# Second sums of a seven written over its raw page, a seventh raw slot, and new constants for the order

## Chip, cores and metric

The kernel runs on one core of one Trainium2 chip. The metric is the device time of one execution in microseconds. Three runs of the kernel before took 2598.05 to 2601.19 us, with a median of 2599.41 us.

## What is computed

Two layers of an encoder over 256 tokens of width 4096, all in float32. Each layer normalises its input, multiplies it by one wide input projection (4096 x 11264), runs grouped attention with rotary embedding on one half of the result and a retention in both directions on the other half, gates both, and multiplies by an output projection (4096 x 4096), which is added to the input. A last normalisation ends it.

```python
for l in range(DEPTH):                       # DEPTH = 2
    h = rmsnorm(x, norm_w[l])
    proj = h @ w_in[l]                       # 256 x 4096 @ 4096 x 11264
    aq, ak, av, ag, rq, rk, rv, rg = jnp.split(proj, SPLIT_POINTS, axis=-1)
    ...
    a_out = (jax.nn.silu(ag) * gqa_attention(aq, ak, av)).astype(x.dtype)
    ...
    r_out = (jax.nn.silu(rg.astype(jnp.float32)) * r).astype(x.dtype)
    x = x + jnp.concatenate([a_out, r_out], axis=-1) @ w_out[l]
return rmsnorm(x, final_norm)
```

## The kernel before

**Products.** Each float32 value is split into a high part and a low part of a shorter type (fp32r): ScalarE (ACT) casts the high part, VectorE (DVE) subtracts it from the value to get the low part. A product is then three matmuls: high by high, low operand by high weight, high operand by low weight. In the profile, `whi` and `wlo` are the parts of a page of weights, and `x8h`, `x8l`, `x7h`, `x7l` those of the operand.

**Blocks.** The work runs in 30 blocks, each over two column groups of 512 (11 of the input projection and 4 of the output projection in each layer). They are numbered from 0; blocks 0, 11, 15 and 26 open the four stages (input and output projection of both layers). In a block, the 4096 rows of the weights are taken in 16 pairs of 2 x 128. Most pairs are "eights" and need eight products of 128 x 128 by 128 x 512 on two pages of weights. Six pairs of each block are "sevens": they use a Strassen-like scheme with seven products, for which sums of the weights are made on the core (`SEVENS`, L130; `SEVEN_PRODUCTS`, L192 on).

**Pages of a seven.** A seven has four pages, used in the order A, T, B, U, with pages of eights between them:
- A is the raw page (`wraw`), loaded from HBM: two halves of 512 columns.
- T is `wv`: a copy of the raw page by ACT, to which a DMA of GpSimd's queue (POOL) adds a prepared array (`add_up`, L690; `add`, L726).
- B is a half page, `third`, loaded from HBM on SyncE's queue (SP) (`load_third`, L546).
- U is `wu`: two sums by DVE. The first is the raw page's second half plus the first half of `wv`; the second is the first sum plus `third`. They are made when page T begins (`begin`, L636), into a tile of their own with one buffer.

Each page is then split: `parts` (L602) casts the high part and leaves the low part to be done later (`low`, kept in `later`); what is given as `then` is called once the low part is issued.

**Raw slots.** There are `RAWS` = 6 slots of 128 x 1024 float32 for raw pages. `load` (L524) puts the next raw page in the oldest free slot, by a DMA on SP's queue (L531). `empty` (L541) hands a slot back and calls `load`. The page of an eight hands its slot back after its low part, the A page of a seven after the second sum of `wu`. At the start all slots are filled before the third chunk of `xT` is loaded (`first_rows`, L1933, called in the opening). Casts are kept in a ring of 5 pages (`RING`), low parts in 4 (`LOWS`).

**Order.** The order of all instructions on each engine is fixed when the program is built: a planner written in the kernel keeps a clock of its own (`Now`, `Clock`, L293 on) with assumed costs and decides, after each product, which splits, loads and steps of the side work (attention, retention, gates, sums, residuals, operand splits) come next (`tick`, L1067; `room`, L731; `Lane`, L977; `block`, L1543). Its constants stand in `BASE` and, for single blocks, in `PLANS` (L111); `assume` (L124) sets those of a block. In `block` the constant `RUSH` is read first, and only if the block is called as hurried (the first of an output projection), and `assume` is called for the block after that.

Of the kernel before, what the change touches and what calls it, by code (L numbers as in the profile page):

```python
# [17 lines left out]
P = 128  # L18
# [9 lines left out]
NB = 512  # L28
# [5 lines left out]
BLK = 32  # L34
ALL = slice(None)
PAGES = 13
RAWS = 6
A_EARLY = 0
SUMS = 2
LOWS = 4  # L40
# [4 lines left out]
STRICT = 4  # L45
RELIEF = 1.5
# [6 lines left out]
STEP_V = 2.0  # L53
STEP_S = 1.5

V_FIXED = 0.1
STT = 0.0
S_FIXED = 0.2

MM = {512: 0.2268, 256: 0.1177}  # L60
PASS = 0.2
# [4 lines left out]
MARGIN = 0.2  # L66
# [4 lines left out]
ADD_SLACK = 0.3  # L71
RAW_SLACK = 0.3
U_SLACK = 0.3
THIRD_SLACK = 0.3
SUM_SLACK = 0.3

RUSH = 1.0

EARLY = 1.3
# [5 lines left out]
PE_REST = 1.5  # L85

TIGHT_A = 2
TIGHT_B = 9

AT_ONCE = 2  # L90
# [9 lines left out]
LOW_AHEAD = 1.5  # L100
LONG = 4
NEAR = 30
# [6 lines left out]
)  # L109
BASE = {_n: globals()[_n] for _n in TUNED}  # L110
PLANS = {  # L111
    1: {'LOW_AHEAD': 5.0},
    6: {'TIGHT_A': 8},
    7: {'SUM_SLACK': 0.0, 'AT_ONCE': 1, 'STRICT': 4},
    8: {'TIGHT_B': 5, 'STRICT': 5},
    9: {'THIRD_SLACK': 1.0, 'BANK_REST': 1.5, 'LOW_AHEAD': 1.0, 'RAW_SLACK': 1.0, 'RELIEF': 0.7, 'PASS': 0.1},
    14: {'STRICT': 9, 'TIGHT_A': 0},
    15: {'S_FIXED': 0.16, 'LONG': 2, 'EARLY': 1.8, 'PASS': 0.3, 'PE_REST': 2.0, 'NEAR': 30},
    22: {'PASS': 0.3, 'U_SLACK': 1.0, 'AT_ONCE': 1},
    24: {'V_FIXED': 0.12, 'TIGHT_B': 20, 'TIGHT_A': 2},  # L120
}


# [169 lines left out]
class Now:  # L293


    t = 0.0
# [40 lines left out]
def hybrid_encoder(  # L337
# [21 lines left out]
    wp = ctx.enter_context(tc.tile_pool(name="wp", bufs=3))  # L359
# [12 lines left out]
    def t(pool, shape, tag, bufs=None, dt=F32):  # L372
        kw = {} if bufs is None else {"bufs": bufs}
        return pool.tile(shape, dt, tag=tag, name=tag, **kw)
# [106 lines left out]
    class Weights:  # L481


        def __init__(self):
# [29 lines left out]
            for i, g in enumerate(self.raws):  # L514
                if g.seven and i > RAWS + A_EARLY:
                    self.raws.insert(i - A_EARLY, self.raws.pop(i))
            self.slots = [f"wraw{_i}" for _i in range(RAWS)]
            self.placed, self.emptied, self.made = 0, 0, 0
# [117 lines left out]
        def begin(self, g):  # L636

            g.begun = True
            if not g.seven:
                ac.after(g.raw_at)  # L640
                self.parts(g, g.raw, then=partial(self.empty, g))
                return
            o = g.own
            if g.kind == PAGE_A:
                self.wanted = max(self.wanted, self.sevens.index(o) + 1)
                self.load_third()
                ac.after(o.a_at)
                self.parts(g, o.a)
            elif g.kind == PAGE_T:
                self.sums_low(PAGE_A)  # L650
                self.sums_low(PAGE_U)
                self.add_up(o)
                self.add(True)
                u = o.u = t(wp, [P, 2, NB], "wu", 1)
                ve.after(max(o.v_at, o.b_at))
                ve.tensor_add(u[:, 0, :], o.a[:, 1, :], o.v[:, 0, :])
                ve.tensor_add(u[:, 1, :], u[:, 0, :], o.b)
                o.u_at = ve.until
                self.empty(next(v for v in self.seq if v.own is o))
                ac.after(o.v_at)  # L660
                self.parts(g, o.v, then=self.spend)
                self.halve()
            else:
                ac.after(o.u_at)
                self.parts(g, o.u)

        def third_split(self):
            self.split_thirds += 1
# [1427 lines left out]
```

## Time and profile before

| | |
|---|---|
| median of 3 runs | 2599.41 us |
| the profiled execution's own time | 2599.34 us |
| its span in the trace | 2597.6 us |
| granted clock | 0.998 |
| DMA | 653.52 MB, 252 GB/s in the mean |

The profile names engines PE (TensorE matmul), PEld (its weight loads), DVE, ACT, POOL and SP. A row of a group reads: line, engine, operation, tile written from tiles read, shapes, count, busy time and mean time of one. L321 is the planner's recorder, through which all operations of DVE and ACT pass, so one goes by tiles there. A row of waits reads: engine, line and tile that waited, what ended the wait, then the sum in us, how often, and the longest. A matmul's end is modelled in the trace: two that follow each other overlap, so the distance from start to start tells the rate, not the length of one.

### The profile page before, as it was taken

To read this page: it belongs to the slowest core of one execution; us is meant where nothing else is said; L and a number is where in the kernel's file an instruction comes from. 1 tells how busy PE (TensorE), PEld (TensorE's weight loads), DVE (VectorE), ACT (ScalarE), POOL (GpSimd) and SP (SyncE) were. 2 spreads that over 40 slices of the span, in tenths; PEclk is the share of its full clock that TensorE was granted. 3 is DMA by queue.
4 is the path that set the end of the run, shared out by engine and by line. 5 is a ranking of instruction groups with operands and counts; after the bars stand their busy time and mean duration, and the time that the engine had idled before them with its cause. 6 is when DMAs were issued, how large, how long until landed. Compare 5 with 4: busy or idle time off the path is not lost.

```text
span 2597.6 us, 34368 instructions
## 1 busy us (share of the span) xinstructions
PE 2581.8 (99%) x11560; PEld 2135.2 (82%) x11560; DVE 2215.3 (85%) x2710; ACT 1853.6 (71%) x2626; POOL 398.6 (15%) x548
## 2 busy tenths in 40 slices
PE   9999999999999999999999999999999999999998
PEld 7888888888888888888878888888888888888886
DVE  7898888888789898777979888889888798987777
ACT  8877777766666788656887667776666667886655
POOL 0111221221102100211111112221201021000000
PEclk9999999999999999999999999999999999999999
DMA  9988988888778778988888879888887787788886
GB/s 314 305 237 277 289 242 254 281 247 263 221 220 260 230 235 227 271 269 248 275 253 261 250 239 279 246 270 268 259 257 222 208 259 242 220 229 251 250 243 194
DMA packets 206594, 653.52 MB, mean 252 GB/s; under 512 B 24784, under 2 KB 31440, under 8 KB 206416
## 3 DMA queue, kind: packets, MB, share of 16 engines
q1 hardware_dynamic: 147040, 472.99, 51.8%
q0 software_dynamic: 58656, 177.24, 30.7%
q8 instruction: 90, 1.47, 0.2%
q10 hardware_dynamic: 720, 1.10, 0.1%
q14 instruction: 88, 0.72, 0.1%
HBM read 607.19 MB, written 44.04 MB: 251 GB/s over the span
## 4 chain that ended last, share of the span: by engine, by line
PE 94%; DMA 2%; DVE 2%; ACT 1%; issue 1%; SPq 0%; DVEq 0%; POOLq 0%; POOL 0%; ACTq 0%
PE M L1683 60%; PE M L1693 30%; PE M L1158 1%; PE M L1157 1%; PE M L1156 1%; DMA ca<-in_x 1%; DVE wlo L321 1%; ACT whi L321 1%; DMA third<-in_w_out 0%; PE M L1677 0%; DMA wraw<-in_w_out 0%; DVE cb L321 0%; DMA whole<-in_w_in 0%; ACT ca L321 0%; DVE ca L321 0%
## 5 line engine op out<-in xcount | busy, mean ns | idle before, releaser
L321 DVE TENSOR_TENSOR wlo<-wraw,whi 128x1024 fp32r<-128x1024 f32 (+1 forms) x774 | 935.3, 1215 | 172.8 <-issue 61.2
L321 ACT CAST whi<-wraw 128x1024 fp32r<-128x1024 f32 (+1 forms) x776 | 800.1, 1045 | 297.1 <-PE M L1683 283.0
L1683 PE MATMUL M<-whi,x8h 128*128 128x512 f32 x2368 | 922.5, 390 | 1.0 <-DVE cb L321 0.8
L1683 PE MATMUL M<-whi,x8l 128*128 128x512 f32 x2368 | 921.8, 389 | 0.0
L1693 PE MATMUL M<-wlo,x8h 128*128 128x512 f32 x2364 | 676.3, 389 | 0.2 <-DVE wlo L321 0.2
L1683 PEld LDWEIGHTS M<-whi,x8h 128*128 128x128 f32 x2368 | 444.6, 188 | 94.9 <-DVE cb L321 1.5
L1683 PEld LDWEIGHTS M<-whi,x8l 128*128 128x128 f32 x2368 | 444.6, 188 | 92.4 <-DVE x8l L321 0.3
L1693 PEld LDWEIGHTS M<-wlo,x8h 128*128 128x128 f32 x2364 | 442.2, 188 | 91.4 <-DVE wlo L321 1.0
L1683 PE MATMUL M<-whi,x7h 128*128 128x512 f32 x1080 | 420.5, 389 | 0.2 <-ACT whi L321 0.2
L1683 PE MATMUL M<-whi,x7l 128*128 128x512 f32 x1080 | 420.3, 389 | 0.0
L1693 PE MATMUL M<-wlo,x7h 128*128 128x512 f32 x1080 | 334.4, 390 | 0.7 <-DVE wlo L321 0.6
L729 POOL DMA_DIRECT2D wv<-in_twice_in x132 | 118.5, 898 | 1068.6 <-ACT wv L321 923.8
L321 ACT CAST whi<-wu 128x1024 fp32r<-128x1024 f32 x180 | 189.3, 1052 | 91.9 <-DVE wu L321 54.2
L321 ACT CAST whi<-wv 128x1024 fp32r<-128x1024 f32 x180 | 189.0, 1050 | 91.5 <-PE M L1683 51.9
L321 DVE TENSOR_TENSOR wlo<-wv,whi 128x1024 fp32r<-128x1024 f32 x180 | 219.6, 1220 | 37.3 <-PE M L1693 30.7
L321 ACT COPY wv<-wraw 128x1024 f32<-128x1024 f32 x180 | 188.9, 1049 | 74.7 <-DMA wraw<-in_w_out 35.2
L321 DVE TENSOR_TENSOR wlo<-wu,whi 128x1024 fp32r<-128x1024 f32 x180 | 219.1, 1217 | 24.8 <-PE M L1693 16.7
L1693 PEld LDWEIGHTS M<-wlo,x7h 128*128 128x128 f32 x1080 | 202.4, 188 | 44.1 <-DVE wlo L321 2.5
L1683 PEld LDWEIGHTS M<-whi,x7h 128*128 128x128 f32 x1080 | 202.8, 188 | 42.6 <-ACT whi L321 0.9
L1683 PEld LDWEIGHTS M<-whi,x7l 128*128 128x128 f32 x1080 | 202.8, 188 | 41.8
L321 DVE TENSOR_TENSOR wu<-wu,third 128x512 f32<-128x512 f32 x180 | 124.6, 692 | 7.0 <-DMA third<-in_w_in 0.8
L321 DVE TENSOR_TENSOR wu<-wraw,wv 128x512 f32<-128x512 f32 x180 | 123.1, 684 | 8.7 <-DMA wv<-in_twice_in 6.3
(249 smaller groups left out, 2292.0 us busy)
## 6 DMA issues: line engine op xcount, KB each, us to landing
wraw<-in_w_in SPq DMA_DIRECT2D x568, 512.0 KB, 5.2
wraw<-in_w_out SPq DMA_DIRECT2D x208, 512.0 KB, 5.4
wv<-in_twice_in POOLq DMA_DIRECT2D x132, 512.0 KB, 7.5
third<-in_w_in SPq DMA_DIRECT2D x132, 256.0 KB, 5.8
wv<-in_twice_out POOLq DMA_DIRECT2D x48, 512.0 KB, 8.1
third<-in_w_out SPq DMA_DIRECT2D x48, 256.0 KB, 5.7
full<-next_dram POOLq DMA_DIRECT2D x18, 512.0 KB, 9.5
p_dram<-room POOLq DMA_DIRECT2D x64, 128.0 KB, 3.4
```

What stands on the lines that cost most here:

```text
L321: return call(out, *args, **kwargs)
L729: self.adds.pop(0)[1]()
L1156: nc.tensor.matmul(out, a[0], b[0], start=start, stop=False)
L1157: nc.tensor.matmul(out, a[0], b[1], start=False, stop=False)
L1158: nc.tensor.matmul(out, a[1], b[0], start=False, stop=stop)
L1683: nc.tensor.matmul(acc[name], a[i], g.hi[h], start=m == first[name] and not i, stop=False)
L1693: nc.tensor.matmul(acc[name], a, g.lo[h], start=False, stop=m == final[name])
```

## The change

The two sums of page U are written into the raw page of the same seven; the tile `wu` is gone. The first sum overwrites the raw page's first half and reads its second, the second sum overwrites the second half. The raw slot of the seven is handed back after the low part of page U, no longer after the second sum. `RAWS` goes from 6 to 7, so that the raw slots take the room that the tile `wu` had. The constants of the planner for single blocks are others for blocks 0, 1, 3, 10, 11, 15, 17, 18, 25 and 26; blocks 6, 7, 8, 9, 14, 22 and 24 keep theirs, and the rest have the base.

```diff
-RAWS = 6
+RAWS = 7
...
 PLANS = {
-    1: {'LOW_AHEAD': 5.0},
+    0: {'EARLY': 1.8, 'RELIEF': 0.7, 'TIGHT_A': 2, 'RAW_SLACK': 0.3},
+    1: {'LOW_AHEAD': 3.0, 'ADD_SLACK': 1.0, 'SUM_SLACK': 0.0, 'U_SLACK': 0.3, 'NEAR': 30},
+    3: {'EARLY': 0.8, 'RAW_SLACK': 3.0},
...
+    10: {'NEAR': 30, 'RAW_SLACK': 0.3, 'STRICT': 6, 'AT_ONCE': 1, 'PE_REST': 2.5, 'THIRD_SLACK': 0.3, 'V_FIXED': 0.12, 'STEP_V': 2.5, 'PASS': 0.2, 'TIGHT_A': 8, 'MARGIN': 0.0},
+    11: {'EARLY': 1.3, 'S_FIXED': 0.18},
     14: {'STRICT': 9, 'TIGHT_A': 0},
-    15: {'S_FIXED': 0.16, 'LONG': 2, 'EARLY': 1.8, 'PASS': 0.3, 'PE_REST': 2.0, 'NEAR': 30},
+    15: {'RUSH': 0.0},
+    17: {'V_FIXED': 0.12},
+    18: {'U_SLACK': 1.0, 'STEP_S': 1.0},
...
+    25: {'STEP_S': 1.0, 'RAW_SLACK': 0.3, 'TIGHT_A': 0, 'SUM_SLACK': 1.0},
+    26: {'NEAR': 40, 'STT': 0.05, 'LONG': 0, 'THIRD_SLACK': 0.3, 'SUM_SLACK': 0.0, 'TIGHT_A': 0, 'EARLY': 1.3, 'V_FIXED': 0.1, 'PASS': 0.2},
 }
...
             elif g.kind == PAGE_T:
...
-                u = o.u = t(wp, [P, 2, NB], "wu", 1)
+                u = o.u = o.a
                 ve.after(max(o.v_at, o.b_at))
                 ve.tensor_add(u[:, 0, :], o.a[:, 1, :], o.v[:, 0, :])
                 ve.tensor_add(u[:, 1, :], u[:, 0, :], o.b)
                 o.u_at = ve.until
-                self.empty(next(v for v in self.seq if v.own is o))
                 ac.after(o.v_at)
                 self.parts(g, o.v, then=self.spend)
                 self.halve()
             else:
                 ac.after(o.u_at)
-                self.parts(g, o.u)
+                self.parts(g, o.u, then=partial(self.empty, next(v for v in self.seq if v.own is o)))
```

## Prediction

> **What bounds the kernel now.** I read the page's totals first, then the chain that ended last, then a table of PE by stretches, and only then who waits for whom.
>
> ```profile
> span 2597.6 us, 34368 instructions
> PE 2581.8 (99%) x11560; PEld 2135.2 (82%) x11560; DVE 2215.3 (85%) x2710; ACT 1853.6 (71%) x2626; POOL 398.6 (15%) x548
> PE 94%; DMA 2%; DVE 2%; ACT 1%; issue 1%; SPq 0%; DVEq 0%; POOLq 0%; POOL 0%; ACTq 0%
> ```
>
> TensorE is busy for 2581.8 of 2597.6 us and holds 94% of the chain. A busy PE isn't yet a PE at its peak, so the next look is at the rate: one piece of the chain, and from the windows view the stretches that matter (columns: PE, weight loads, DVE, ACT, POOL, each with its count, then the granted clock, the DMA share and GB/s).
>
> ```profile
> 1350.74 1.81 PE M L1683 x8
> 0.00:88.00 88.00, 86.29 (x351) 65.10 (x352) 71.42 (x103) 74.29 (x116) 5.56 (x10) 1.00 0.92 310
> 953.00:1040.00 87.00, 87.00 (x400) 72.59 (x399) 77.62 (x104) 72.55 (x115) 6.72 (x8) 1.00 0.76 218
> 1127.00:1214.00 87.00, 87.00 (x385) 72.04 (x384) 68.35 (x72) 53.04 (x61) 14.41 (x20) 1.00 0.86 258
> 1214.00:1300.00 86.00, 85.55 (x376) 69.99 (x375) 75.40 (x104) 70.47 (x114) 17.12 (x25) 1.00 0.91 287
> 1300.00:1390.00 90.00, 88.90 (x385) 71.45 (x384) 74.97 (x95) 72.47 (x114) 11.03 (x14) 1.00 0.85 250
> 2248.00:2335.00 87.00, 87.00 (x396) 72.15 (x395) 78.76 (x106) 71.07 (x111) 9.05 (x9) 1.00 0.75 220
> 2510.00:2572.00 62.00, 61.39 (x271) 50.39 (x270) 49.27 (x58) 41.27 (x58) 4.36 (x5) 1.00 0.84 250
> ```
>
> Eight matmuls took 1.81 us, 0.2267 us each. In 1127:1214, 385 matmuls touch the stretch, some 1.5 of them only over its edges: 383.5 x 0.2267 = 86.9 of 87 us, so nothing is lost there. The same count gives, for 1300:1390, 383.5 x 0.2267 = 86.9 of 90 us, **3.1 us lost**; for 1214:1300, 374.5 x 0.2267 = 84.9 of 86, **1.1 us lost**; for 2510:2572, 269.5 x 0.2267 = 61.1 of 62, **0.9 us lost**. Outside the first 88 us and the tail, that is all I find: 5.1 us. Few of them show as waits of PE with a name:
>
> ```profile
> PE M L1693 <- DVE wlo L321: 0.8, 2, 0.6
> PE M L1683 <- DVE cb L321: 0.8, 1, 0.8
> PE M L1683 <- DVE ca L321: 0.2, 1, 0.2
> PE M L1683 <- ACT whi L321: 0.2, 1, 0.2
> ```
>
> So TensorE waits for splits (whi, wlo) and for bank sums (ca, cb), never for a raw page directly. The change touches no matmul, so **5.1 us is about what it can win** in the stretches above, 0.196% of 2599.34 us, the profiled execution's time, which is 0.07 us off the median of 2599.41. The execution lies 1.7 us over its span, and I keep that.
>
> **The change part by part.** The sums come first. Two rows of the view of their tile (ns least, median, most; first and last start), and one of the waits:
>
> ```profile
> L321 DVE TENSOR_TENSOR wu<-wraw,wv x180: 651/684/694, 26.8 to 2564.6; 128x512 f32<-128x512 f32 x180
> L321 DVE TENSOR_TENSOR wlo<-wu,whi x180: 1180/1218/1228, 31.7 to 2570.1; 128x1024 fp32r<-128x1024 f32 x180
> ...
> DVE wu L321 <- DMA wv<-in_twice_in: 6.3, 4, 2.7
> ```
>
> Nothing is removed or added in number: 2 x 180 sums, 180 casts, 180 lows stay, with the same shapes. I cost the sums' new place at 0: they run on DVE behind the A page's low, and their input wv comes from a copy that ACT made of the same raw page, so every reader of the raw page is done when the sum may start anyway. The old wait that goes is that of a new wu for the cast and the low of the last one; what the sums do wait for is wv's landing (the last row, 6.3 us in all, from the view of waits), and that stays.
>
> What moves is the **raw load that follows a seven**. Before, its slot comes free after the second sum; now after the U page's low. From the first and the last row (26.8 to 31.7 + 1.2, and 2564.6 to 2570.1 + 1.2) the room is taken for 6.1 and 6.7 us, about 6.4 x 180 = 1150 us, 44% of the span if the ones between are alike. In that time there are six slots for raw pages as before, in the rest seven. The wait it adds stands on SP's queue, in front of the next raw and third loads:
>
> ```profile
> SPq L531 <- DVE wlo L321: 1343.6, 541, 7.9
> SPq L531 <- DVE wu L321: 606.3, 175, 9.0
> wraw<-in_w_in SPq DMA_DIRECT2D x568, 512.0 KB, 5.2
> wraw<-in_w_out SPq DMA_DIRECT2D x208, 512.0 KB, 5.4
> ```
>
> SP already waits for DVE before nearly every load, and the load is issued in the program where its release is, so the 175 waits for a sum become waits for a low, later on both sides. 776 loads in 2597.6 us are one in 3.35 us; six slots turn round in 20.1 us, seven in 23.4. A load lands in 5.2 to 5.4 us. The gain is up to 3.35 us of earlier issue for a raw page that comes late. Who feels a late one:
>
> ```profile
> ACT wv L321 <- DMA wraw<-in_w_out: 35.2, 17, 6.4
> ACT wv L321 <- DMA wraw<-in_w_in: 32.9, 25, 3.8
> ACT whi L321 <- PE M L1683: 362.0, 393, 3.9
> DVE wlo L321 <- PE M L1693: 95.8, 122, 1.6
> ```
>
> ACT waited 68.1 us for raw pages in all, but 362.0 us in 393 waits for TensorE to free a cast: over the span the casts run to the end of their ring, which hides late raws. Not so where TensorE loses time (ACT's waits in 1214:1300, 1300:1390, 1390:1476, 2510:2572; each fence a window):
>
> ```profile
> ACT wv L321 <- DMA wraw<-in_w_out: 7.0, 3, 4.2
> ACT whi L321 <- PE M L1683: 3.7, 4, 2.5
> ```
> ```profile
> ACT whi L321 <- PE M L1683: 3.0, 3, 2.1
> ACT wv L321 <- DMA wraw<-in_w_in: 0.9, 1, 0.9
> ```
> ```profile
> ACT whi L321 <- PE M L1683: 18.1, 21, 3.9
> ```
> ```profile
> ACT wv L321 <- DMA wraw<-in_w_out: 8.5, 3, 6.4
> ACT whi L321 <- PE M L1683: 5.1, 7, 2.3
> ```
>
> In the first and the last of them raws were late by 7.0 and 8.5 us with little ring ahead; in 1300:1390 they were not. So the seventh slot can win between 0 and 0.9 + 1.1 = 2.0 us. For the last stretch I take all 0.9: its longest wait of 6.4 us halves with 3.35 us. For 1214:1300 I take 0.5 of 1.1, since DVE is busy for 75.4 of 86 us there. **Term: -1.4 us.** What is late next in both is DVE's own turn.
>
> The slots are also filled at the start, by one more load ahead of the third chunk of xT.
>
> ```profile
> 6.16 3.54 SPq L531 DMA_DIRECT2D wraw<-in_w_in  x4
> 10.64 1.61 SPq L1937 DMA_DIRECT2D full<-in_xT  x2
> 21.50 0.90 ACT L321 ACTIVATE full<-full,nw 128x256 f32<-128x256 f32 x2
> ```
>
> At 310 GB/s of the first stretch 512 KB cost 1.7 us. The chunk is first scaled at 21.50, and TensorE is then still in the two native pairs and pairs 3 and 2. **Bounds 0 to +1.7 us; I take 0**, because about 9 us of matmuls (two pairs) lie between; without them it costs the 1.7.
>
> A rule speaks against the extra load: the Trainium skill, "DMA: Bandwidth & Descriptors", section "Queues, rings and completion order", says that each DMA engine takes turns between the queues that have work. By it a further raw load on SP's queue slows the accumulations and residuals of POOL's queue, and the sum would be that of the contention rival below. No row here separates the queues' turns.
>
> The **orders**: new constants for blocks 0, 1, 3, 10, 11, 15, 17, 18, 25, 26. Block 15's own five go; what comes, RUSH, is read before the block's constants are set and only in hurried blocks, so block 15 runs on the base. Blocks 0, 11, 15 and 26 open the four stages, and there the splits of the operand share ACT and DVE with those of the weights. What an order costs, 1300:1390 shows:
>
> ```profile
> 1328.76 0.82 ACT L321 COPY ca<-room 32x256 f32<-32x256 f32 x2
> 1329.60 1.05 ACT L321 CAST whi<-wu 128x1024 fp32r<-128x1024 f32 x1
> 1330.69 1.23 DVE L321 TENSOR_TENSOR wlo<-wu,whi 128x1024 fp32r<-128x1024 f32 x1 [1.44 <-ACT whi L321]
> 1382.15 0.50 PE L1683 MATMUL M<-whi,x8h 128*128 128x512 f32 x1 [0.80 <-DVE cb L321]
> ```
>
> Pieces of 0.4 us went ahead of a cast that TensorE needed. A new order can take these 3.1 us away or bring as many at another opening: bounds -3.1 and, per opening, +3.1. Nearest is the row itself, a stretch that is as full as before: I take 0. Sum: 2599.34 - 1.4 = **2597.9 us**.
>
> **Rivals.** *No relief:* the lost time is DVE's and ACT's crowding, not raws; four of PE's named waits are all on them. Then 2599.3, or up to 2601.0 with the start's 1.7. *All of it goes:* 2599.34 - 5.1 = 2594.2; for it, no named wait of TensorE is over 0.8 us; against it, DVE and ACT stand at 83% and 81% in 1300:1390. *Contention:* POOL's transfers land later by one load's 1.7 us where TensorE has no ring ahead, once in 1214:1390: 2601.0. Against it, the bytes stay the same. *Slower, by the openings:* the new orders put operand splits ahead of the weights' at openings that lose nothing now (953:1040 and 2248:2335 are 87.00 of 87). Each that becomes like 1300:1390 costs 3.1 us; one more is +3.1 (2602.4), from two on, +6.2 (2605.5), it is over the bound, all three (blocks 0, 11, 26) give 2608.6. For it: ACT there is busy for 72.55 and 71.07 of 87 us, as full as in 1300:1390. Against it: they lost nothing under a like load.
>
> By the Trainium skill, "TensorE: Matmul & The Clock Gate", section "HAM oscillation — how this bites in real kernels", an idle stretch of TensorE beyond some 3.4 us drops its clock to half, so that a loss of an opening in one piece would cost more than its length. The granted clock is 1.00 in all rows above, with no wait over 0.8 us, so no run here shows it.
>
> **How the numbers follow.** Forecast (2595.5 to 2599): 0.45. No relief (to 2602): 0.20. Contention: 0.08. All of it goes (2594.2 to 2595.5): 0.08. Slower by the openings: 0.16. Faster than the 5.1 us allow, by a shorter start or tail too: 0.03. A measurement can tell about 0.2%, 5.2 us, from no change, so the first four are "same": 0.81; slower 0.16, faster 0.03. The range leaves out the last two: 2594.2 to 2604.6, from the 5.1 us won to just over one opening lost with the start's 1.7 (2604.1).
>
> **What would show it.** Right: PE 99% with 11560 matmuls; the wait of ACT for in_w_out raws in the last stretch well under 8.5 us and the stretch's loss near 0; first sums with wraw as output, 180 of some 684 ns; SP's waits for a sum gone, waits for wlo up. Wrong on orders: a stretch of 87 us around 953 or 2248 with some 14 matmuls too few. Wrong on the start: a gap of PE between 26 and 40 us. The prediction falls if TensorE's time per matmul moves, or if stretches that lost nothing now lose more than 5 us together.

## The result, and the profile after

| | median, us | runs |
|---|---|---|
| before | 2599.25 | 13, 2597.41 to 2601.19 |
| after | 2604.76 | 13, 2603.00 to 2606.91 |

The ratio is **1.0022, interval 1.0014 to 1.0030**: the change costs about 5.5 us, where 1.4 us less were forecast. The profiled execution's span went from 2597.6 to 2603.0 us, so it shows the whole of the loss.

The page of the kernel after: span, busy times, and the shares of the chain that ended last.

```profile
span 2603.0 us, 34347 instructions
PE 2583.7 (99%) x11560; PEld 2134.8 (82%) x11560; DVE 2225.5 (85%) x2710; ACT 1854.9 (71%) x2627; POOL 396.5 (15%) x548
PE 94%; DVE 2%; DMA 2%; ACT 1%; issue 1%; SPq 0%; POOL 0%; POOLq 0%; DVEq 0%; ACTq 0%
L329 DVE TENSOR_TENSOR wraw<-wraw,third 128x512 f32<-128x512 f32 x180 | 124.6, 692 | 9.3 <-DMA third<-in_w_in 3.2
L329 DVE TENSOR_TENSOR wraw<-wraw,wv 128x512 f32<-128x512 f32 x180 | 123.9, 688 | 4.2
```

Nothing here tells where 5.4 us went. PE is 99% busy as before, and its busy time grew by 1.9 us only; the work is the same 11560 matmuls. The two sums are there with their new output, at 688 and 692 ns each, as in a tile of their own. The stretches tell more, by the count of matmuls as in the prediction.

Windows view of the kernel after, the same stretches as before (columns: PE, weight loads, DVE, ACT, POOL, granted clock, DMA share, GB/s):

```profile
0.00:88.00 88.00, 85.16 (x339) 62.55 (x340) 68.62 (x100) 72.14 (x115) 5.53 (x10) 1.00 0.90 299
953.00:1040.00 87.00, 87.00 (x402) 72.72 (x401) 78.42 (x109) 73.43 (x120) 6.67 (x8) 1.00 0.74 214
1214.00:1300.00 86.00, 85.67 (x375) 69.67 (x374) 74.46 (x104) 69.77 (x112) 16.16 (x23) 1.00 0.93 288
1300.00:1390.00 90.00, 85.75 (x373) 69.12 (x372) 73.66 (x93) 71.31 (x116) 8.90 (x11) 1.00 0.84 236
2248.00:2335.00 87.00, 87.00 (x398) 72.10 (x397) 77.83 (x104) 72.08 (x114) 6.71 (x8) 1.00 0.75 217
2510.00:2572.00 62.00, 62.00 (x275) 51.36 (x274) 48.61 (x55) 41.67 (x55) 6.07 (x7) 1.00 0.91 265
```

The first 88 us hold 339 matmuls in place of 351: 12 x 0.2267 = **2.7 us**. In 1300:1390 it is (373 - 1.5) x 0.2267 = 84.2 of 90 us, **5.8 us lost** in place of 3.1. The openings of blocks 11 and 26, around 953 and 2248, lost nothing. In 2510:2572 the loss seems gone (ACT's waits for raw pages there fell from 8.5 to 4.9 us), but it only moved past the edge, to a wait at 2577 (below).

The waits of PE in the kernel after, the whole span (engine, line and tile that waited, what ended it, sum, times, longest):

```profile
PE M L1690 <- ACT x8h L329: 2.5, 1, 2.5
PE M L1700 <- DVE wlo L329: 2.2, 5, 1.0
PE M L1690 <- ACT whi L329: 1.5, 1, 1.5
```

Before, no named wait of TensorE for a split or a sum was over 0.8 us; now two single ones are 2.5 and 1.5. The timeline of the kernel after places them (start, length, engine, line, operation; in brackets the idle time before it and who ended it):

```profile
22.83 0.91 ACT L329 ACTIVATE full<-full,nw 128x256 f32<-128x256 f32 x2 [1.04 <-DMA full<-in_xT]
...
42.79 0.73 PE L1700 MATMUL M<-wlo,x7h 128*128 128x512 f32 x2 [1.04 <-DVE wlo L329]
...
1316.32 1.05 ACT L329 COPY wv<-wraw 128x1024 f32<-128x1024 f32 x1 [4.85 <-DMA wraw<-in_w_in]
1317.28 1.04 ACT L329 CAST whi<-wraw 128x1024 fp32r<-128x1024 f32 x1
1318.37 0.50 PE L1690 MATMUL M<-whi,x8h 128*128 128x512 f32 x1 [1.53 <-ACT whi L329]
...
1366.53 1.65 ACT L329 COPY cb<-room 32x256 f32<-32x256 f32 x4
...
1370.62 1.04 ACT L329 CAST whi<-wraw 128x1024 fp32r<-128x1024 f32 x1
...
1372.38 0.70 ACT L329 CAST x8h<-cb 128x256 fp32r<-128x256 f32 x2
1373.13 0.51 PE L1690 MATMUL M<-whi,x8h 128*128 128x512 f32 x1 [2.47 <-ACT x8h L329]
...
2577.33 0.73 PE L1700 MATMUL M<-wlo,x7h 128*128 128x512 f32 x2 [0.57 <-DVE wlo L329]
```

Two places, then. **At the start** the scaling of the third chunk of xT begins at 22.83 in place of 21.50 us, and ACT idles 1.04 us for its landing; some 20 us later TensorE waits for the low parts. By the starts of the matmuls 0.5 us is lost between 29 and 34 us, 1.3 at 42.79, 0.5 at 56 and 0.3 around 75. **At the layer boundary** ACT stands 4.85 us in front of a copy to wv, because the raw page has not landed, and the cast that TensorE needs is queued behind that copy: TensorE stops for 1.53 us. From 1366.53 on four copies to cb and then four casts of weights, the last at 1370.62, go ahead of the operand's cast x8h: TensorE stops for 2.47 us. In the kernel before, x8h goes ahead of those four casts; its timeline there:

```profile
1365.20 0.70 ACT L321 CAST x8h<-cb 128x256 fp32r<-128x256 f32 x2
1367.22 1.05 ACT L321 CAST whi<-wraw 128x1024 fp32r<-128x1024 f32 x1
```

The first of the two waits at the boundary is led back by the chain of the kernel after, cut to 1295:1320:

```profile
1304.93 11.31 DMA wraw<-in_w_in
...
1316.32 0.04 ACT wv L329
```

A raw load issued at 1304.93 took 11.31 us; the median of all raw loads of this kernel is 5.2 to 5.3. At this place long ones are usual: of the raw loads in 1290:1320 the median is 6.2 and the longest is this one, and before they were 6.6 and 10.6. So the landing alone isn't the cause, but that the copy which waits for it has a needed cast behind it. The planner counts with 6.0 us from its estimate of the issue (`RAW_LANDING`); the copy and the cast behind it were placed by that belief.

As a ruler for all that follows I use the start of the same-numbered matmul in each trace (a matmul of one number is the same product in all kernels), less that of before:

```
matmul   before, us   after
   360        90.08   +2.84
  5000      1117.51   +2.82
  5700      1276.17   +3.33
  6000      1346.95   +4.28
  6250      1404.99   +5.93
 11000      2457.60   +6.11
 11559      2585.32   +5.97
```

So 2.8 us are lost in the first 90 us, 0.5 by 1276, another 2.6 by 1405, and from there on nothing that counts. One trace of each kernel carries this. For one kernel traced twice (e5 and e11 below) the ruler's readings differed by up to 0.6 us, so a step smaller than that isn't read from one trace alone. The ruler also holds time in which TensorE's clock was halved behind a wait (last section): the traces of e1, e2, e3, e4, e9 and e12 have such stretches, those of before, after, e5 to e8, e10 and e11 have none before the last matmuls.

### The profile page after: what moved, and what is told of

Read it like the earlier page. It is cut to its first block, busy times and chain, and to the rows that moved or that the text cites. A ratio compares the mean times of both kernels' runs of the same rounds, so it can differ in the third digit from the quotient of the medians.

```text
span 2603.0 us, 34347 instructions
## 1 busy us (share of the span) xinstructions
PE 2583.7 (99%) x11560; PEld 2134.8 (82%) x11560; DVE 2225.5 (85%) x2710; ACT 1854.9 (71%) x2627; POOL 396.5 (15%) x548
## 4 chain that ended last, share of the span: by engine, by line
PE 94%; DVE 2%; DMA 2%; ACT 1%; issue 1%; SPq 0%; POOL 0%; POOLq 0%; DVEq 0%; ACTq 0%
PE M L1690 61%; PE M L1700 30%; DMA wraw<-in_w_in 1%; PE M L1165 1%; PE M L1164 1%; PE M L1163 1%; DVE wlo L329 1%; ACT whi L329 1%; DMA full<-in_xT 0%; DVE cb L329 0%; DVE ca L329 0%; ACT cb L329 0%; DVE xf L329 0%; ACT full L329 0%; DVE x7l L329 0%
## 5 line engine op out<-in xcount | busy, mean ns | idle before, releaser
L329 DVE TENSOR_TENSOR wlo<-wraw,whi 128x1024 fp32r<-128x1024 f32 x954 | 1148.9, 1216 | 197.0 <-PE M L1700 75.3
L329 ACT CAST whi<-wraw 128x1024 fp32r<-128x1024 f32 x956 | 983.7, 1046 | 389.5 <-PE M L1690 308.5
L329 DVE TENSOR_TENSOR wraw<-wraw,third 128x512 f32<-128x512 f32 x180 | 124.6, 692 | 9.3 <-DMA third<-in_w_in 3.2
L329 DVE TENSOR_TENSOR wraw<-wraw,wv 128x512 f32<-128x512 f32 x180 | 123.9, 688 | 4.2
L329 ACT CAST bhi<-third 128x512 fp32r<-128x512 f32 x180 | 111.3, 618 | 20.3 <-PE M L1690 15.1
L329 DVE TENSOR_TENSOR blo<-third,bhi 128x512 fp32r<-128x512 f32 x180 | 123.1, 684 | 0.0
```

Source lines behind the costliest of these rows:

```text
L329: return call(out, *args, **kwargs)
```

## The experiments

Four parts of the change can carry the loss: the sums' place (in the raw page), the longer hold of the slot, the extra load ahead of xT, and the order that the planner makes from seven slots and new constants. The theory after the result was: the extra load at the start, and the order at block 15. Its rivals were the slots' traffic in general and the constants alone.

**e1: the third xT chunk ahead of the seventh raw.** Only SP's order changes.

```diff
-    while weights.slots:
+    while len(weights.slots) > 1:
         weights.load()
     first_rows(2)
+    weights.load()
```

> The changed kernel, with the third chunk of xT loaded ahead of the seventh raw page at the start and nothing else moved on any engine. Theory A (the start's 2.8 us come from the extra load ahead of xT): ACT no longer idles 1.04 us for the chunk at 22.8 us, the first 90 us come back to those of before, time 2602.0 us. Theory B (they come from the new order of block 0): the chunk lands earlier but TensorE still loses 2.8 us by 90 us, time 2604.8 us.

Measured: 2605.41 us, ratio 1.0025 (1.0015 to 1.0036). That is theory B's time: no gain, and the ruler reads +2.77 at matmul 360, as in the kernel after. The timeline of e1 tells why:

```profile
21.62 0.91 ACT L329 ACTIVATE full<-full,nw 128x256 f32<-128x256 f32 x2
29.26 0.69 DVE L329 TENSOR_TENSOR wraw<-wraw,third 128x512 f32<-128x512 f32 x1 [1.61 <-DMA third<-in_w_in]
```

The scaling is back at 21.62, but the raw load now stands ahead of the next thing in that queue, the first third, and DVE waits 1.61 us for it. The lateness was passed on, not removed. e1 thus doesn't speak against the load as the cause; e8 asks the question better.

**e2 and e3: code and constants apart.** e2 is the code of after with the `PLANS` of before, e3 the code of before with the `PLANS` of after.

```diff
 e2, in the code of after
-    0: {'EARLY': 1.8, 'RELIEF': 0.7, 'TIGHT_A': 2, 'RAW_SLACK': 0.3},
-    1: {'LOW_AHEAD': 3.0, 'ADD_SLACK': 1.0, 'SUM_SLACK': 0.0, 'U_SLACK': 0.3, 'NEAR': 30},
+    1: {'LOW_AHEAD': 5.0},
...
-    15: {'RUSH': 0.0},
+    15: {'S_FIXED': 0.16, 'LONG': 2, 'EARLY': 1.8, 'PASS': 0.3, 'PE_REST': 2.0, 'NEAR': 30},
...
```

> The changed kernel (sums in the raw page, seven slots) with the constants of before. Theory A (start from the load, layer boundary from the new constants of blocks 14 to 15): the start still loses 2 to 3 us, 1214 to 1390 us loses some 4 us as before and not 7, time 2602 us. Theory B (all from the orders): 2599 us. Theory C (all from the slots): 2604.8 us.

> The kernel before (tile wu, six slots) with the new constants. Theory A (start from the load, boundary from the constants): nothing lost at the start, 3 us more than before lost around 1300 us, time 2602 us. Theory B (all from the orders): 2604.8 us. Theory C (all from the slots): 2599.3 us.

Measured: e2 2615.67 us, ratio 1.0065 (1.0048 to 1.0082); e3 2607.20 us, ratio 1.0033 (1.0019 to 1.0046). Each half alone is slower than before, e2 is the slowest kernel of all, and no theory had either time. Where e2 loses, the windows view of e2 and its waits of PE say:

```profile
953.00:1040.00 87.00, 83.88 (x376) 69.26 (x375) 75.20 (x106) 70.78 (x113) 6.71 (x8) 0.98 0.71 209
1300.00:1390.00 90.00, 84.49 (x362) 67.22 (x363) 71.64 (x92) 73.68 (x118) 9.53 (x12) 1.00 0.81 233
2248.00:2335.00 87.00, 83.97 (x379) 69.19 (x378) 76.46 (x107) 70.94 (x116) 6.70 (x8) 0.98 0.73 206
```
```profile
PE M L1682 <- ACT whi L321: 3.9, 2, 2.8
PE M L1682 <- DVE ca L321: 2.9, 2, 2.6
PE M L1692 <- DVE blo L321: 2.1, 1, 2.1
```

376 in place of 400 matmuls around 953 (24 x 0.2267 = 5.4 us) and 362 in place of 385 in 1300:1390 (5.2 us). In 2248:2335 17 are missing against before, 3.9 us. In the first and the last of these stretches TensorE also ran at half clock for 3.4 us behind a wait; 8 matmuls touch such a piece where 16 fit, so up to 1.8 us of each loss is the clock's. The new constants thus repair, around blocks 11 and 26, what the planner does worse once it is told of seven slots and a later release. They are no gain in themselves: with six slots, in e3, they cost 8 to 9 us. Part of that lies at the start: at matmul 360 the ruler reads +4.97 in e3, and +3.90 in e10 (below), which has the same order and no halved clock there. Neither has an extra load at the start.

**e4: block 15's old constants in the kernel after.**

```diff
-    15: {'RUSH': 0.0},
+    15: {'S_FIXED': 0.16, 'LONG': 2, 'EARLY': 1.8, 'PASS': 0.3, 'PE_REST': 2.0, 'NEAR': 30},
```

> The changed kernel with the old constants of block 15 alone. Theory A1 (block 15 on the base puts casts, residual work and operand splits in a worse order): the two waits of TensorE at 1317 and 1371 us, 4.3 us, shrink to under 2 us, time 2602 us. Theory A2 (it is the late landing of one raw page at 1316 us, made before block 15's constants matter): both stay, time 2604.8 us.

Measured: 2605.13 us, ratio 1.0023 (1.0013 to 1.0033), no change against after. The ruler reads +2.81 at 5700, +7.64 at 6000 and +7.99 at 6250: the same place loses more. Part of that is the clock: the wait for whi is 2.9 us here, and behind it TensorE ran at half clock for 6.8 us. Block 15's constants alone aren't the cure.

**e5, e6, e7: the slots without a new order.** The kernel before, with its order kept on every engine: the planner is told of six slots and books its loads as before, while the program has seven. The sums go into the raw page. The load behind a seven is issued where it stood, but into the spare slot, which the last seven's page U has left, so it waits for no sum. In e6 each load goes out as soon as a slot is free, one page ahead of the planner's booking, and the seventh ahead of xT, as in the kernel after; in e7 only from the first release on. SP's own order in e5 is that of before too.

```diff
+LOGICAL = 6
...
+        def fill(self):
+            while self.slots and self.put < min(self.placed + self.ahead, len(self.raws)):
+                g = self.raws[self.put]
...
+                nc.sync.dma_start(g.raw, g.src)
...
-                u = o.u = t(wp, [P, 2, NB], "wu", 1)
+                u = o.u = o.a
...
-                self.empty(next(v for v in self.seq if v.own is o))
+                self.load()
...
-                self.parts(g, o.u)
+                self.parts(g, o.u, then=partial(self.spare, next(v for v in self.seq if v.own is o)))
...
 e6, in the opening
+    weights.ahead = 1
+    weights.fill()
     first_rows(2)
```

> Sums in the raw page and seven slots, but every instruction of every engine in the order of the kernel before: the planner is told of six slots and each load is issued where it was, into the slot that the last seven's sums left. Theory D (writing in place costs nothing; the loss comes from the order that the planner makes when it sees seven slots): 2599.3 us, at most 1 us off, nothing lost at the start or at the openings beyond before. Theory E (in place costs something by itself, by waits of the sums or the later release): 2601 to 2605 us, spread over the span.

> As the run before it, but each raw load is issued as soon as a slot is free, up to one page ahead of the order of before, the seventh ahead of the third chunk of xT; PE, ACT, DVE and POOL keep the order of before. Theory F (the extra load in flight delays what lands behind it: xT, thirds, accumulations): 2 to 3 us lost by 90 us, time 2601.5 to 2602 us. Theory D (order alone): 2599.3 us. The hope of the change (late raws were what cost): under 2598.5 us, with the loss of 2510 to 2572 us gone.

> As e6, but six raw loads at the start, and the page ahead only from the first release on. Theory F at the start alone: the first 90 us as before and the rest as in e6, time under 2599.5 us. Theory D: 2599.3 us, same as e5 and e6.

Measured: e5 **2595.86 us, ratio 0.9989** (0.9980 to 0.9998); e6 2598.50, ratio 0.9999 (0.9990 to 1.0008); e7 2597.86, ratio 0.9995 (0.9986 to 1.0004). Sums in place and a seventh slot are thus worth 3 us if the order stays and each load keeps its place in the queue, a gain that neither theory on e5 had. To fetch a page ahead in addition gives most of it back: neither e6 nor e7 can be told from before, and e7's median is 2.0 us over e5's, though the intervals of the ratios overlap. By the ruler e6 stands 1.8 us behind e5 at matmul 4230 (+1.46 in place of -0.31), of which some 1.0 were lost around 170 us, and 3.9 behind at the end. A window and a wait of ACT in e6, in 160:180:

```profile
160.00:180.00 20.00, 19.56 (x86) 15.54 (x85) 19.83 (x31) 13.61 (x23) 2.69 (x2) 1.00 0.62 193
```
```profile
ACT bhi L322 <- DMA third<-in_w_in: 1.4, 1, 1.4
```

ACT waits for a third page, issued at 152.66, to which the chain of e6 leads the loss back; 90 matmuls stood there before, 86 now. That the raw loads ahead of it in SP's queue made it late is likely, not shown: e7 fetches ahead too and lost nothing there.

Where e5 wins shows in SP's waits in 1290:1330, of before and of e5:

```profile
SPq L531 <- DVE wu L321: 22.3, 4, 9.0
SPq L531 <- DVE wlo L321: 17.3, 7, 4.4
```
```profile
SPq L542 <- DVE wlo L322: 32.8, 9, 10.1
```

The waits for a sum, 22.3 us, are gone, and those for a low part grew from 17.3 to 32.8, so that SP waits 32.8 us for the two in place of 39.6. Over the whole span SP's queue is hardly freer: it waits for wlo, wu and blo for 2027.5 us before and for 1975.3 in e5. What moves is when single loads go out. One load as an example, in the timelines of before and of e5:

```profile
1297.22 0.33 SPq L531 DMA_DIRECT2D wraw<-in_w_in  x1
```
```profile
1290.33 0.33 SPq L542 DMA_DIRECT2D wraw<-in_w_in  x1
```

It goes out 6.9 us earlier. The windows view of e5 answers:

```profile
1214.00:1300.00 86.00, 86.00 (x381) 71.25 (x380) 76.84 (x107) 70.42 (x114) 18.42 (x25) 1.00 0.92 290
1300.00:1390.00 90.00, 89.98 (x396) 73.87 (x395) 76.46 (x95) 74.87 (x116) 10.56 (x14) 1.00 0.85 250
2510.00:2572.00 62.00, 61.98 (x273) 50.97 (x272) 52.01 (x62) 40.49 (x55) 3.49 (x4) 1.00 0.71 219
```

In 1300:1390 the loss falls from 3.1 to 90 - (396 - 1.5) x 0.2267 = 0.6 us. The same pieces of ca and cb stand ahead of the same casts as before; the casts in front of them were done earlier, so TensorE had more in hand. Whether it is the earlier page itself that helps, or the loads behind it in the queue, no run separates.

**e8: the seventh page later, in the kernel after.** Its DMA is held back until just before the next raw load, so behind two chunks of xT and the first third. PE, ACT, DVE and POOL keep the order of after.

```diff
+                if self.placed == RAWS:
+                    self.held_back = g
+                else:
+                    self.bring()
+                    nc.sync.dma_start(g.raw, g.src)
```

> The changed kernel with the seventh raw page of the start loaded behind two chunks of xT and the first third; PE, ACT, DVE and POOL keep the changed kernel's order. Theory F (what lands behind the extra load is late, and that is the start's loss; in e1 the lateness only passed from xT to the third): under 1 us lost by 90 us against before, time 2602.5 us. Theory D (the order of block 0 loses them, whatever lands when): 2 to 3 us lost by 90 us as before, time 2604.8 us.

Measured: 2603.93 us, ratio 1.0017 (1.0008 to 1.0026). The intervals of e8 and after overlap, so the time alone doesn't carry it; the trace does. Its timeline at the place of the 22.83 above:

```profile
21.22 0.91 ACT L329 ACTIVATE full<-full,nw 128x256 f32<-128x256 f32 x2
```

The scaling starts 1.61 us earlier, and the ruler reads +1.17 in place of +2.84 at matmul 360. **1.7 us of the start are the extra load**; the other 1.2 stay with no load in the way, and are left to the order of block 0. Other traces repeat both: with the load in its place e4 and e9 read +2.71 and +2.73, without it e12 reads +1.21. The 1.2 us come in steps at 42, 56 and 75 us, and the first two, of 0.4 to 0.7 us each, stand also in e3 and e10, which have the new constants of block 0 and no extra load.

With the order of before, in e6, the same extra load costs 0.4 to 0.7 us by matmul 360 (+0.43, where e7, e11 and e5 read +0.04, -0.07 and -0.31). There the scaling starts at 21.99, only 0.5 to 0.8 us later than in those three. So in both orders TensorE loses about what the chunk is late; why it is less late in e6 isn't shown.

**e9: the copy to wv later, in block 15 of the kernel after.** The copy is planned 3 us behind the believed landing, so the casts behind it pass it; 14 rows of ACT move and some five of DVE, none of PE.

```diff
+SUM_LATE = 0.0
...
-    15: {'RUSH': 0.0},
+    15: {'SUM_LATE': 3.0},
...
-                elif not o.a or o.a_at > now.t or ...
+                elif not o.a or o.a_at + SUM_LATE > now.t or ...
```

> The changed kernel; in block 15 ACT takes the copy of a seven's raw page only 3 us after the planner believes that it landed, so that a late page does not stop the casts behind the copy. ACT's order changes in some 14 rows around 1310 to 1370 us, PE's not at all. Theory G (ACT standing 4.9 us at 1316 us for one raw page sets the waits at 1317 and 1371 us): both shrink, 2 to 4 us come back, time 2601 to 2603 us. Theory H (ACT and DVE are simply full there): the wait moves to another cast or operand, time 2604 to 2605 us.

Measured: 2604.25 us, ratio 1.0017 (1.0008 to 1.0027). The waits of PE in e9:

```profile
PE M L1691 <- ACT x8h L330: 2.7, 1, 2.7
PE M L1701 <- DVE wlo L330: 1.6, 3, 1.1
```

By the time alone that is theory H. But the wait for whi (1.53 us) is gone, and the ruler falls to +0.34 at matmul 6000, 3.9 us better than after: 1.8 of that are there at matmul 5800, ahead of the copy, and 1.9 more come by 5900, behind it. At 6250 it is +3.82 again, 2.1 better than after: the next wait, for x8h, grew from 2.5 to 2.7 us, and TensorE's clock was halved behind it (last section). So the queueing at 1316 is shown as a cause in the trace, of some 2 us, and e12 repeats it against e8 (2.2 us between matmuls 5800 and 5900); the wait for x8h takes back 1.8. The copies to cb don't make that wait in e9, where the last of them end at 1361.03. Its timeline shows what stands ahead of x8h, four casts of weights from here on, the first of which waited for a landing:

```profile
1363.98 1.05 ACT L330 CAST whi<-wv 128x1024 fp32r<-128x1024 f32 x1 [0.94 <-DMA wv<-in_twice_in]
...
1368.63 0.71 ACT L330 CAST x8h<-cb 128x256 fp32r<-128x256 f32 x2
```

The place of x8h behind the casts of weights is what e9 and the kernel after share; no run moved x8h alone.

**e10: the order of e3 with the edit of e5.** A new order, six slots in the planner's mind, sums in place. e10 and e3 differ as e5 and before do.

```diff
 in the code of e3
-RAWS = 6
+RAWS = 7
+LOGICAL = 6
...
-                u = o.u = t(wp, [P, 2, NB], "wu", 1)
+                u = o.u = o.a
...
```

> The order of e3 (six-slot planner, new constants) with sums in the raw page and the load behind a seven issued into the spare slot at once, as e5 did for the order of before. Theory J (that a load need not wait for the sums is worth something in any order): 1.5 to 4 us under e3's 2607.2, time 2603 to 2605.7 us. Theory K (e5's gain is peculiar to the order of before): 2607 us.

Measured: 2603.56 us, ratio 1.0017 (1.0008 to 1.0026), against 1.0033 for e3. That is theory J: sums in the raw page and loads that need not wait for a sum gain 0.16%, about 4 us (the intervals of the two ratios overlap at their ends; the ruler reads +4.48 against +9.22 at matmul 11559, but e3's trace has two stretches at half clock in that and e10's none). The order of e3, with all that, stays 4 us behind before and 8 behind e5.

**e11: e5 once more**, since it is the only kernel that is faster than before.

> e5 a second time, beside the runs above: theory D with loads that no longer wait for sums: 2595.9 us, 2 to 4 us under before; had e5's gain been chance, 2599 us.

Measured: **2595.68 us, ratio 0.9984** (0.9975 to 0.9993). The gain holds, 3 to 4 us.

**e12: e8 and e9 together.** If start and boundary are two causes, their gains add up.

> The changed kernel with both local edits: the seventh raw page of the start loaded behind the first third (e8), and the copies of block 15 taken 3 us later (e9). If the start's late landings and the copy that waits for a late page are separate causes, their gains in the traces add, 1.7 us by 90 us and 2.4 us at the layer boundary: 2604.8 - 4.1 = 2600.7 us, and what is left above before (the order of block 0, the operand split that comes late at 1367 us) is still there. If a delay at the start only shifts the same wait, 2603 to 2604 us.

Measured: 2602.24 us, ratio 1.0013 (1.0004 to 1.0022). The median is 2.8 us over before in place of after's 5.5, between the two theories; the intervals still overlap. In the traces the gains add: +1.21 at matmul 360 (after +2.84, e8 +1.17), -0.47 at 6000 (after +4.28), and a span of 2599.4 us, 3.6 below after's, where e8 alone gave 0.9 and e9 alone 2.3. The halved clock at the x8h wait is there again.

## Why the prediction was wrong

**What bounds the kernel** held: TensorE's time per matmul didn't move, and the losses were found as missing matmuls in single stretches. The condition under which the prediction was to fall came near: the first 88 us lost 2.7 us more than before, and 1300:1390, which had lost 3.1, another 2.7.

**The sums at no cost** held: 180 at 688 and 180 at 692 ns, against 684 and 692 before; e5, with its sums in the raw page, is no slower; and SP's waits for a sum became waits for a low part, as forecast (1343.6 + 606.3 us for the two before). The longest row of SP's waits in the kernel after:

```profile
SPq L539 <- DVE wlo L329: 1828.9, 715, 9.6
```

**The term of the later raws**, -1.4 us, had the right sign, and its size hangs on when the loads go out. With the order kept and a page fetched ahead, e7, without the start's load, stands 0.05% under before, some 1.3 us, which can't be told from 0 or from -1.4. With each load in its old place e5 and e11 measured -3 and -4 us (0.11% and 0.16% of 2599), and e10 against e3 about the same. The place was half wrong. Of 1214:1300 the prediction took 0.5 of 1.1 us, and in e5 it is gone altogether (381 matmuls fill the 86 us); of the last stretch's 0.9 half is gone, not all. Most came in 1300:1390, where I had seen no late raws in ACT's waits and so looked for none; what the earlier raws gave there was casts in advance.

**"The start: bounds 0 to +1.7; I take 0, because about 9 us of matmuls lie between" failed.** The bound was right: 1.7 us in e8. The cover wasn't. Matmuls lie between, but the lateness passed through ACT and DVE to TensorE undiminished: 1.61 us at the scaling, 1.67 at matmul 360 (after against e8), one time by xT and, in e1, one time by the third. At 42.79 TensorE took a low part that DVE had finished only 0.05 us before. Of the sign that I named, a loss of PE between 26 and 40 us, 0.5 us was there; the long gap came at 42.79.

**"The orders: bounds -3.1 and, per opening, +3.1 ... I take 0" failed, and this is the larger part.** e6 has the slots, the sums and the early loads of after, in the order of before: ratio 0.9999. After has 1.0022. So the order that the planner made anew costs 0.23%, about **6 us**. By the ruler 2.4 of them lie in the first 90 us (+2.84 against +0.43): 1.2 are block 0's order by itself, the rest that xT comes later than in e6. Another 4.0 lie at the layer boundary, between matmuls 5700 and 6250, where after loses 2.6 and e6 gains 1.4: before's own waits at 1331 and 1382 went there, and new ones of 1.53 and 2.47 us came at 1317 and 1371. The rival "slower, by the openings" had the mechanism (pieces ahead of a cast that TensorE needs) and with one opening plus the start, 2604.1, nearly the time; I held it at 0.16. That its time came so near is in part luck, for its places were wrong: blocks 11 and 26, which it looked at first, lost nothing (e2 loses there, so the new constants mend just these); blocks 0 and 15 lost, and 15's stretch had lost 3.1 us already. My reason against it, "they lost nothing under a like load", says nothing of an order not yet seen: a busy share of 82% doesn't tell which instruction stands in front.

**What stays open.** Why block 0's order costs 1.2 us without the load wasn't isolated. Nor was the wait for x8h: no run moved that cast alone, and in e4, with the old constants of block 15, it is 0.7 us, but behind a longer wait and a halved clock. Why the load at 1304.93 took 11.31 us isn't shown either; it ran while loads of the residuals (ca and cb from in_x, issued at 1302.93 and 1303.65) ran on POOL's queue, which would be the contention that the prediction weighed, but before had such loads and late raws there too, and no kernel was run without them. The order of after with a tile wu of its own wasn't tried.

## What to carry to other kernels

A change of buffers in a kernel whose order is planned is two changes: run the new buffers in the old order first (e5), then the new order by itself, for constants fit only the state they were chosen in (the same arithmetic took 2595.7 to 2615.7 us here). Cost an earlier load by what stands behind it in its queue, and its cover by the finished work that the engines in between hold in advance, not by the matmuls between; at this start it was next to none. And look for an engine's instruction that waits for a transfer with a needed one behind it: one late landing of 11 us with a cast behind it cost some 2 us here, more than half of what the extra slot won in e5.

## What was not expected of the hardware

TensorE's clock was halved behind single waits of 1.8 to 2.9 us, and once behind two short ones. In the traces' records of the granted clock every stretch but the last is a whole number of steps of 3.413 us: in e9 1365.33 us at 1.00 (400 steps), 3.41 at 0.50 (one), 1218.56 at 1.00 (357). So each trace can be cut into steps. The windows views of e9, of after and of e3, cut at their steps (the column after POOL's is the granted clock; the first count is the matmuls that touch the step, 16 in a full one):

```profile
1366.81:1370.22 3.41, 0.83 (x3) 0.48 (x3) 2.73 (x5) 3.41 (x9) 0.00 (x0) 1.00 0.44 168
1370.22:1373.64 3.42, 3.42 (x10) 2.68 (x9) 1.41 (x3) 1.17 (x3) 0.00 (x0) 0.50 0.45 157
1373.64:1377.05 3.41, 3.41 (x16) 2.81 (x15) 1.23 (x1) 1.31 (x2) 0.00 (x0) 1.00 0.15 30
```
```profile
1368.36:1371.78 3.42, 2.30 (x11) 1.56 (x9) 3.18 (x5) 3.42 (x5) 0.00 (x0) 1.00 0.55 162
1371.78:1375.19 3.41, 2.06 (x8) 1.50 (x9) 2.37 (x4) 3.41 (x8) 0.00 (x0) 1.00 0.40 150
```
```profile
75.16:78.58 3.42, 1.77 (x6) 0.84 (x6) 3.38 (x5) 3.42 (x6) 0.00 (x0) 1.00 0.45 165
78.58:81.99 3.41, 3.41 (x9) 2.63 (x9) 3.38 (x5) 3.09 (x5) 0.00 (x0) 0.50 0.44 138
```

In e9 the wait for x8h, 2.67 us, falls almost whole into one step, and the next step runs at half clock: 10 matmuls touch it where 16 fit, 1.4 us lost on top of the wait. After's wait of 2.47 us is cut in two by the end of a step, and the clock stays at 1.00. e3's two short waits (0.73 and 0.80 us) fall into one step and halve the clock; in e10 the same two are parted by the end of a step at 77.43, and the clock stays. So the length of a wait alone doesn't decide: it depends on how much of one step is idle. Between 20 us and the last matmuls the traces hold eight halvings, each behind a step that 3 to 7 matmuls touch. No step with 8 or more was followed by one, and of the four with 7 two were (e1, e2) and two weren't (e2, e10). In e4 the halved clock lasted two steps.

The Trainium skill, "TensorE: Matmul & The Clock Gate", section "HAM oscillation — how this bites in real kernels", puts the edge at idle gaps of more than some 3.4 us. Here shorter ones, and even two short ones together, were enough; the measurement decides, and what the rule adds in kind, that the drop costs time beyond the gap, is as it says.
